# Written engine orders for the first 17 and last 16 slots of a matmul with decayed cumulative sum

## The chip, the cores and the metric

One core of one Trainium2 chip. The metric is device time in microseconds (us), the median of several executions. PE is the matrix engine (PEld its weight loads), DVE the vector engine, ACT the scalar engine, POOL GpSimd, SP the engine that issues the stores.

## The reference

```python
# x: (16, 2048, 1024), w: (1024, 1024), decay: (1024,), all float32
xw = x @ w
out[:, 0, :] = xw[:, 0, :]
for t in range(1, 2048):
    out[:, t, :] = decay * out[:, t - 1, :] + xw[:, t, :]
```

## The kernel before

The 16 x 2048 rows of x are 64 chunks of 512 rows. A chunk is loaded by GpSimd (cast to bf16), turned by DVE (32x32 transposes) and copied by ACT into the layout that PE reads (tile `xt`). Two chunks form a group; a *slot* is one block n of 128 output columns of a group, 2 x 8 matmuls of 512 columns into one PSUM tile of 1024. There are three such PSUM tiles, so PE can be at most two slots ahead of whoever empties the oldest. Each slot's recurrence runs over time inside the tile. A *direct* slot is one DVE scan over all 1024 steps. A *paired* slot combines two neighbouring steps so that DVE scans only 512, at the price of work on ACT and GpSimd:

```python
        def pair(self):          # "P"
            ...
            pin(nc.scalar.copy(out=self.xs, in_=self.ps))
            g = self.decayed(self.ps[:, 0:T:2])          # ACT: times decay; PSUM is free after it
            ... # first element of so: memset, or the state of the chunk before
            pin(nc.gpsimd.tensor_tensor(
                out=self.xs[:, 1:T:2], in0=g, in1=self.xs[:, 1:T:2], op=ALU.add))
        def scan(self):          # "S": DVE, 512 steps from xs, or 1024 steps straight from PSUM
            ...
        def complete(self):      # "C": ACT decays the odd steps, GpSimd adds the even ones; keep the state
            ...
        def back(self):          # "B": DVE turns the result; after the last of four blocks, store()
            ...
```

Every fourth slot is direct (from PSUM), the others are paired; only in the last eight slots, of one chunk each, is every second direct, and the last but one too. One rule orders the engines, slot after slot, start and end like the middle:

```python
    steps = {2: (3, 3, 4), 3: (4, 5, 5), 4: (7, 8, 10)}    # turn and copies of chunks 2, 3, 4
    def behind(new):
        if new is not None: new.pair()
        before = waiting[-1] if waiting else None
        if before is not None and before.paired: before.scan()
        if new is not None and not new.paired: new.scan()
        if before is not None: before.complete()
        ...                       # then back() of the slot before, or of the one before that
    slots = [(g, n) for g in groups[:-1] for n in range(K)]
    slots += [(groups[-1], n) for n in range(R)]            # R = 4, K = 8
    slots += [([c], n) for c in groups[-1] for n in range(R, K)]
```

All engines run strictly in the order written: `pin` keeps the program's order.

Of the kernel before, what the change touches and what calls it, by code (L numbers as in the profile page):

```python
# [25 lines left out]
def kernel(  # L26
# [7 lines left out]

# [102 lines left out]
    class Tile:  # L137
# [3 lines left out]
        def __init__(self, g, n, ps, ot):  # L141
            self.b, self.t0 = chunks[g[0]]
            self.T = TL * len(g)
            self.n, self.ps, self.ot = n, ps, ot
            self.final = g == [nch - 1]
            if len(g) == 2:
                self.paired = n % R != R - 1
            else:
                self.paired = n % 2 == 0 and not (self.final and n == K - 2)
# [65 lines left out]
        def back(self):  # L215
            T, n = self.T, self.n
            pin(nc.vector.transpose(  # L217
                out=self.ot[:, :, n % R * P:(n % R + 1) * P],
                in_=self.so[:, 2:T + 2].rearrange("p (i t) -> p i t", t=P)))
            if self.final:  # L220
                if n % 2:
                    self.store(n - 1, n + 1)
            elif n % R == R - 1:
                self.store(n + 1 - R, n + 1)

        def store(self, n0, n1):
            c0 = n0 % R * P
            size = (n1 - n0) * P
            for q in (0, 2, 1, 3):
# [9 lines left out]
    stage = {(0, 0): room[0][:, 0:size],  # L239
             (0, 1): room[0][:, size:size * 3 // 2].bitcast(BF16),  # L240
             (1, 0): room[1][:, 0:size // 2].bitcast(BF16),
             (1, 1): room[1][:, size // 2:size].bitcast(BF16)}

    def load_w(queue, h, e):
        for q in range(NQ):
            pin(queue.dma_start(  # L246
                out=stage[h, e][quad(q)].rearrange("p (m d) -> p m d", m=M),
                in_=_ap(w, [[2 * D, P], [2 * P * D, M], [1, CH]],
                        (q * CQ + e) * D + h * CH)))

    def settle(h, e, m, copy):
        src = stage[h, e][:, m * CH:(m + 1) * CH]
# [12 lines left out]
    load_w(nc.sync, 0, 0)  # L265
# [4 lines left out]
    for j0, j1 in halves:  # L270
        for q in range(NQ):
            load(0, q, j0, j1)
    load_w(nc.gpsimd, 0, 1)
    for j0, j1 in halves:
        for q in range(NQ):
            load(1, q, j0, j1)
    load_w(nc.gpsimd, 1, 0)
    load_w(nc.gpsimd, 1, 1)
    for q in range(NQ):
        load(2, q)  # L280

    def enter(c, j0, j1):
        turn(c, j0, j1)
        part(c, nc.vector.tensor_copy, 0, 2, j0, j1)
        part(c, nc.scalar.copy, 2, M, j0, j1)

    for e in range(2):
        for m in range(M):
            settle(0, e, m, nc.vector.tensor_copy if m < M // 2 else nc.scalar.copy)
        if e == 0:  # L290
            for j0, j1 in halves:
                enter(0, j0, j1)
    cols = const.tile([128, 2, P], FP32, name="cols")
    pin(nc.vector.transpose(out=cols, in_=rows))
    pin(nc.vector.tensor_copy(
        out=dec.rearrange("p (h r) -> p h r", h=2), in_=cols[:, :, 0:R]))
    pin(nc.vector.tensor_tensor(out=dec2[:, 0:K], in0=dec, in1=dec, op=ALU.mult))
    for j0, j1 in halves:
        enter(1, j0, j1)
    for m in range(M):  # L300
        settle(1, 0, m, nc.vector.tensor_copy)


    agenda = {}
    loads = []

    def at(step, f, *args):
        agenda.setdefault(step, []).append(lambda: f(*args))
# [6 lines left out]
    for m in range(M):  # L315
        at(0, settle, 1, 1, m, nc.vector.tensor_copy)
    steps = {2: (3, 3, 4), 3: (4, 5, 5), 4: (7, 8, 10)}
    for gi, g in enumerate(groups):
        for l, c in enumerate(g):
            if c > 1:  # L320
                ahead = (-7, -6, -4) if l else (-11, -10, -8)
                when = steps.get(c, [gi * K + s for s in ahead])
                at(when[0], turn_and_load, c)
                at(when[1], part, c, nc.scalar.copy, 0, 2)
                at(when[2], part, c, nc.scalar.copy, 2, M)

    waiting = []

    def behind(new):

        if new is not None:
            new.pair()
        before = waiting[-1] if waiting else None
        if before is not None and before.paired:
            before.scan()
        if new is not None and not new.paired:
            new.scan()
        if before is not None:
            before.complete()
        waiting.append(new)  # L340
        if len(waiting) == 4:
            waiting.pop(0)
        for tl, lag in ((waiting[0] if len(waiting) == 3 else None, True),
                        (before, False)):
            if tl is not None and tl.paired == lag:
                tl.back()

    loads.extend((c, q) for c in (3, 4) for q in range(NQ))
    slots = [(g, n) for g in groups[:-1] for n in range(K)]
    slots += [(groups[-1], n) for n in range(R)]  # L350
    slots += [([c], n) for c in groups[-1] for n in range(R, K)]
    for step, (g, n) in enumerate(slots):
        T = TL * len(g)
        if n % R == 0:
            ot = ot_tile(NJ * len(g))
        if step == 0:
# [9 lines left out]
            for j0, j1 in halves:  # L366
                for i in range(2):
# [20 lines left out]
        for f in agenda.pop(step, []):  # L388
            f()
# [34 lines left out]
```

## Time and profile before

| | before |
|---|---|
| time, median (range) | 928.25 us (928.22 to 928.48) |
| span of the profiled run | 926.5 us |
| PE busy | 893.3 us (96%) |
| first real matmul, last matmul's end | 12.81, 912.47 |
| waits of PE between 20 and 77 us | 11.6 us |
| DVE's last transpose ends | 918.62 |

The lines behind this table are in the prediction. How to read them: a timeline line is start, length, engine, source line, operation, output<-inputs, shapes, count; in brackets stands how long the engine stood idle before and what ended it. A line of the stretches is the window, its length, then busy time (and count) of PE, PEld, DVE, ACT, POOL, then PE's granted clock (1 is full), DMA share (1 is all 16 engines busy) and GB/s.

### The profile page before, as it was taken

To read this page: it belongs to the slowest core of one execution; us is meant where nothing else is said; L and a number is where in the kernel's file an instruction comes from. 1 tells how busy PE (TensorE), PEld (TensorE's weight loads), DVE (VectorE), ACT (ScalarE), POOL (GpSimd) and SP (SyncE) were. 2 spreads that over 40 slices of the span, in tenths; PEclk is the share of its full clock that TensorE was granted. 3 is DMA by queue.
4 is the path that set the end of the run, shared out by engine and by line. 5 is a ranking of instruction groups with operands and counts; after the bars stand their busy time and mean duration, and the time that the engine had idled before them with its cause. 6 is when DMAs were issued, how large, how long until landed. Compare 5 with 4: busy or idle time off the path is not lost. (4 is left out here: it accounts for less than half of the span.)

```text
span 926.5 us, 11865 instructions
## 1 busy us (share of the span) xinstructions
PE 893.3 (96%) x4080; PEld 408.1 (44%) x4162; DVE 827.9 (89%) x608; ACT 686.2 (74%) x937; POOL 666.6 (72%) x760
## 2 busy tenths in 40 slices
PE   8789999999999999999999999999999999999993
PEld 4334444444444444444444444444444444444441
DVE  4779999999999999999999999999999999999876
ACT  3478787787787787787777777777778778778751
POOL 7678877777776777777777777777777787785561
PEclk9999999999999999999999999999999999999997
DMA  9999999999999999999999999999999999999667
GB/s 184 146 190 229 215 226 247 252 248 242 262 230 222 236 226 222 236 228 222 234 231 220 233 231 223 237 225 229 229 229 225 232 234 222 230 228 193 144 168 181
DMA packets 406124, 204.74 MB, mean 221 GB/s; under 512 B 12848, under 2 KB 405552, under 8 KB 406064
## 3 DMA queue, kind: packets, MB, share of 16 engines
q1 hardware_dynamic: 269040, 135.29, 59.2%
q0 software_dynamic: 137024, 68.70, 55.4%
q8 instruction: 32, 0.52, 0.2%
q14 instruction: 28, 0.23, 0.1%
HBM read 138.42 MB, written 134.22 MB: 294 GB/s over the span
## 5 line engine op out<-in xcount | busy, mean ns | idle before, releaser
L127 PE MATMUL ps<-xt,wsb 128*128 128x512 bf16 (+1 forms) x4018 | 879.1, 378 | 18.0 <-DVE so L196 5.3
L127 PEld LDWEIGHTS <-wsb 128*128 128x128 bf16 x4128 | 404.2, 98 | 496.8 <-issue 18.6
L176 POOL TENSOR_TENSOR xs<-h,xs 128x512 f32<-128x512 f32 x192 | 247.4, 1288 | 206.0 <-ACT h L160 95.4
L170 ACT COPY xs<-ps 128x1024 f32<-128x1024 f32 x192 | 193.0, 1005 | 163.7 <-PE ps L127 155.5
L217 DVE STREAM_TRANSPOSE ot<-so 128x1024 f32<-128x1024 f32 (+1 forms) x260 | 302.4, 1201 | 2.5 <-POOL so L210 1.7
L210 POOL TENSOR_TENSOR so<-h,xs 128x512 f32<-128x512 f32 x192 | 246.5, 1284 | 34.8 <-ACT h L160 22.4
L124 ACT COPY xt<-xw 128x2048 bf16<-128x2048 bf16 (+1 forms) x128 | 240.0, 1876 | 15.1 <-DVE xw L116 15.1
L160 ACT ACTIVATE h<-so,dec 128x512 f32<-128x512 f32 x192 | 147.8, 770 | 39.3 <-DVE so L182 35.7
L106 POOL DMA_DIRECT2D xb<-in_x_dram x264 | 174.4, 661 | 2.3 <-POOLq L408 0.9
L182 DVE TENSOR_TENSOR_SCAN so<-dec,keep,xs 128x512 f32<-128x512 f32 (+1 forms) x96 | 121.3, 1264 | 34.4 <-POOL xs L176 34.2
L182 DVE TENSOR_TENSOR_SCAN so<-dec,xs 128x512 f32<-128x512 f32 x96 | 117.3, 1223 | 38.0 <-POOL xs L176 34.7
L116 DVE STREAM_TRANSPOSE xw<-xb 128x2048 f32<-128x2048 f32 (+1 forms) x66 | 146.6, 2221 | 4.3 <-DMA xb<-in_x_dram 4.3
L160 ACT ACTIVATE h<-ps,dec 128x512 f32<-128x512 f32 x192 | 132.5, 690 | 0.0
L196 DVE TENSOR_TENSOR_SCAN so<-dec,keep,ps 128x1024 f32<-128x1024 f32 (+1 forms) x34 | 75.7, 2228 | 0.0
L196 DVE TENSOR_TENSOR_SCAN so<-dec,ps 128x1024 f32<-128x1024 f32 x31 | 70.1, 2261 | 0.0
L213 ACT COPY keep<-so 128x1 f32<-128x1 f32 x132 | 24.8, 188 | 0.0
L175 ACT COPY so<-keep 128x1 f32<-128x1 f32 x96 | 18.4, 191 | 0.0
L262 PE MATMUL spare<-idle 128*128 128x512 bf16 x34 | 10.3, 479 | 1.2 <-DVE idle L259 1.2
L173 POOL MEMSET so<- 128x1 f32 x96 | 11.3, 117 | 0.0
L246 POOL DMA_DIRECT2D ot<-in_w_dram x12 | 6.7, 560 | 4.2 <-DMA xb<-in_x_dram 2.7
L253 DVE COPY wsb<-ot 128x512 bf16<-128x512 bf16 x10 | 5.4, 595 | 2.8 <-DMA ot<-in_w_dram 2.8
L253 ACT ACT_TABLE_LOAD x1 | 1.3, 1283 | 8.8 <-DMA ot<-in_w_dram 8.8
(18 smaller groups left out, 23.6 us busy)
## 6 DMA issues: line engine op xcount, KB each, us to landing
out_dram<-ot SPq DMA_DIRECT2D x252, 512.0 KB, 10.3
xb<-in_x_dram POOLq DMA_DIRECT2D x248, 256.0 KB, 7.5
xb<-in_x_dram POOLq DMA_DIRECT2D x16, 128.0 KB, 6.1
ot<-in_w_dram POOLq DMA_DIRECT2D x12, 128.0 KB, 5.0
ot<-in_w_dram SPq DMA_DIRECT2D x4, 256.0 KB, 5.2
out_dram<-ot SPq DMA_DIRECT2D x4, 256.0 KB
out_dram<-ot SPq DMA_DIRECT2D x8, 128.0 KB, 3.0
rows<-in_decay_dram SPq DMA_DIRECT2D x4, 1.0 KB
```

The source lines that it names most:

```text
L106: pin(nc.gpsimd.dma_start(out=xb_of[c][quad(q), j0:j1], in_=_ap(x, [[D, P], [P * D, j1 - j0], [1, CQ]], (b * S + t0 + j0 * P) * D + q * CQ)))
L116: pin(nc.vector.transpose(out=dst.rearrange("p (m j i) -> p j m i", m=M, i=P)[:, j0:j1], in_=src.rearrange("p (j m c) -> p j m c", m=M, c=P)))
L124: pin(copy(out=xt_of[c][:, m0:m1, :, j0 * P:j1 * P], in_=src))
L127: pin(nc.tensor.matmul(out=ps[:, t0:t1], lhsT=wsb[:, k, n].rearrange("p q i -> p (q i)"), rhs=xt[:, k // 2, k % 2, t0:t1], start=(k == 0 a ...
L160: pin(nc.scalar.activation(out=h, in_=src, func=mybir.ActivationFunctionType.Copy, scale=dec[:, self.n:self.n + 1]))
L170: pin(nc.scalar.copy(out=self.xs, in_=self.ps))
L176: pin(nc.gpsimd.tensor_tensor(out=self.xs[:, 1:T:2], in0=g, in1=self.xs[:, 1:T:2], op=ALU.add))
L182: pin(nc.vector.tensor_tensor_scan(out=so[:, 3:T + 2:2], data0=dec2[:, n:n + 1].to_broadcast([128, T // 2]), data1=self.xs[:, 1:T:2], init ...
L196: pin(nc.vector.tensor_tensor_scan(out=so[:, t:t + size], data0=dec[:, n:n + 1].to_broadcast([128, size]), data1=ps, initial=before, op0=A ...
L210: pin(nc.gpsimd.tensor_tensor(out=so[:, 2:T + 2:2], in0=h, in1=self.xs[:, 0:T:2], op=ALU.add))
L213: pin(nc.scalar.copy(out=self.keep, in_=so[:, T + 1:T + 2]))
L217: pin(nc.vector.transpose(out=self.ot[:, :, n % R * P:(n % R + 1) * P], in_=self.so[:, 2:T + 2].rearrange("p (i t) -> p i t", t=P)))
```

## The change

The intent is to win the waits at the start and shorten the tail, both of which the one rule for the middle does not suit. The core of the diff:

```diff
-    load_w(nc.sync, 0, 0)                       # first weight block: 1 MB of f32 on SP
+    load_w(nc.sync, 0, 0, 0, M // 2)            # half of it on SP; the other half, cast, on GpSimd ("U0")
-                for i in range(2):              # chunk 1 in half chunks for two heads (blocks 0, 1)
+                for i in range(3):              # ... for three
-            if len(g) == 2:
-                self.paired = n % R != R - 1
-            else:
-                self.paired = n % 2 == 0 and not (self.final and n == K - 2)
+            self.paired = n % R != R - 1
-    slots += [(groups[-1], n) for n in range(R)]
-    slots += [([c], n) for c in groups[-1] for n in range(R, K)]
+    slots += [([c], n) for c in groups[-1] for n in range(K)]
+    flips = (0, 1, -2, -15, -8)                 # slots that change between paired and direct
+    agenda = {
+        -99: "M0 M1 U0 U1 M2 M3 U2 U3 L L L W0 w1 E0 F0 G0 w3 W2 E1 F1 G1 W4 w5 W6 w7 E2 F2 D G2 E3 F3 G3 W8 W9 W10 W11",
+        0: "w12 L L w13 P0 S0",
+        1: "w14 L P1 L",
+        2: "S1 W15 P2 B0 S2",
+        3: "T2 L S3 C0 C1 C2",
+        4: "L P4 X2 L Y2 L B2 T3 B1 L",
         ... (slots 5 to 15)
+        16: "L P16 B14 B15 Y6 L L",
+        -16: "P-16 B-17 S-16 C-16 C-17",
+        -15: "P-15",
+        -14: "S-15 B-18 B-16 P-14",
         ... (slots -13 to -3)
+        -2: "P-2 S-2 C-4 C-3 B-4",
+        -1: "B-3 P-1 S-1 B-2 C-5 B-1 C-1 C-2",
+    }
```

P, S, C, B are the four parts of a slot; L loads a quarter chunk; T turns a chunk on DVE, X and Y are its copies on ACT; W copies a weight piece on DVE, w on ACT; M, E, F, G load, turn and copy half chunks; D prepares the decays. Slot -1 is the last one. P of a direct slot is nothing. All other slots keep the old rule.

More of the change, by code (lines that the diff above doesn't have):

```diff
@@ L137, with __init__ @@
     class Tile:
-        def __init__(self, g, n, ps, ot):
+        def __init__(self, g, n, ps, ot, there):
             self.b, self.t0 = chunks[g[0]]
             self.T = TL * len(g)
-            self.n, self.ps, self.ot = n, ps, ot
+            self.n, self.ps, self.ot, self.there = n, ps, ot, there
             self.final = g == [nch - 1]
-            if len(g) == 2:
-                self.paired = n % R != R - 1
-            else:
-                self.paired = n % 2 == 0 and not (self.final and n == K - 2)
+            self.paired = n % R != R - 1
+            if len(tiles) in flips or len(tiles) - len(slots) in flips:
+                self.paired = not self.paired
             self.so = ring(sb, "so", 4, [128, 2 * TL + 2])
@@ L219, in back @@
                 in_=self.so[:, 2:T + 2].rearrange("p (i t) -> p i t", t=P)))
-            if self.final:
-                if n % 2:
-                    self.store(n - 1, n + 1)
-            elif n % R == R - 1:
-                self.store(n + 1 - R, n + 1)
+            self.there.add(n)
+            size = 2 if self.final and n >= R else R
+            n0 = n // size * size
+            if self.there.issuperset(range(n0, n0 + size)):
+                self.store(n0, n0 + size)
         def store(self, n0, n1):
@@ L238, with load_w @@
     size = M * CH
-    stage = {(0, 0): room[0][:, 0:size],
-             (0, 1): room[0][:, size:size * 3 // 2].bitcast(BF16),
-             (1, 0): room[1][:, 0:size // 2].bitcast(BF16),
-             (1, 1): room[1][:, size // 2:size].bitcast(BF16)}
-    def load_w(queue, h, e):
+    stage = {(0, 0, 0): room[0][:, 0:size // 2],
+             (0, 0, M // 2): room[0][:, size // 2:size * 3 // 4].bitcast(BF16),
+             (0, 1, 0): room[0][:, size:size * 3 // 2].bitcast(BF16),
+             (1, 0, 0): room[1][:, 0:size // 2].bitcast(BF16),
+             (1, 1, 0): room[1][:, size // 2:size].bitcast(BF16)}
+    def load_w(queue, h, e, m0=0, m1=M):
         for q in range(NQ):
             pin(queue.dma_start(
-                out=stage[h, e][quad(q)].rearrange("p (m d) -> p m d", m=M),
-                in_=_ap(w, [[2 * D, P], [2 * P * D, M], [1, CH]],
-                        (q * CQ + e) * D + h * CH)))
+                out=stage[h, e, m0][quad(q)].rearrange("p (m d) -> p m d", m=m1 - m0),
+                in_=_ap(w, [[2 * D, P], [2 * P * D, m1 - m0], [1, CH]],
+                        (q * CQ + m0 * 2 * P + e) * D + h * CH)))
     def settle(h, e, m, copy):
-        src = stage[h, e][:, m * CH:(m + 1) * CH]
+        m0 = M // 2 if (h, e) == (0, 0) and m >= M // 2 else 0
+        src = stage[h, e, m0][:, (m - m0) * CH:(m - m0 + 1) * CH]
         pin(copy(out=wcols[:, 2 * m + e, h],
@@ L269, with load_half, load_part, settle_one @@
             in_=_ap(decay, [[P, R], [CH, 2], [1, P]], q * CR)))
-    for j0, j1 in halves:
+    cols = const.tile([128, 2, P], FP32, name="cols")
+    def load_half(i):
         for q in range(NQ):
-            load(0, q, j0, j1)
-    load_w(nc.gpsimd, 0, 1)
-    for j0, j1 in halves:
-        for q in range(NQ):
-            load(1, q, j0, j1)
-    load_w(nc.gpsimd, 1, 0)
-    load_w(nc.gpsimd, 1, 1)
-    for q in range(NQ):
-        load(2, q)
-    def enter(c, j0, j1):
-        turn(c, j0, j1)
-        part(c, nc.vector.tensor_copy, 0, 2, j0, j1)
-        part(c, nc.scalar.copy, 2, M, j0, j1)
-    for e in range(2):
-        for m in range(M):
-            settle(0, e, m, nc.vector.tensor_copy if m < M // 2 else nc.scalar.copy)
-        if e == 0:
-            for j0, j1 in halves:
-                enter(0, j0, j1)
-    cols = const.tile([128, 2, P], FP32, name="cols")
-    pin(nc.vector.transpose(out=cols, in_=rows))
-    pin(nc.vector.tensor_copy(
-        out=dec.rearrange("p (h r) -> p h r", h=2), in_=cols[:, :, 0:R]))
-    pin(nc.vector.tensor_tensor(out=dec2[:, 0:K], in0=dec, in1=dec, op=ALU.mult))
-    for j0, j1 in halves:
-        enter(1, j0, j1)
-    for m in range(M):
-        settle(1, 0, m, nc.vector.tensor_copy)
-    agenda = {}
-    loads = []
-    def at(step, f, *args):
-        agenda.setdefault(step, []).append(lambda: f(*args))
+            load(i // 2, q, *halves[i % 2])
+    def load_part(i):
+        load_w(nc.gpsimd, *((0, 0, M // 2, M), (0, 1), (1, 0), (1, 1))[i])
+    def settle_one(i, copy):
+        settle(i // 8, i // 4 % 2, i % 4, copy)
+    def decays(i):
+        pin(nc.vector.transpose(out=cols, in_=rows))
+        pin(nc.vector.tensor_copy(
+            out=dec.rearrange("p (h r) -> p h r", h=2), in_=cols[:, :, 0:R]))
+        pin(nc.vector.tensor_tensor(out=dec2[:, 0:K], in0=dec, in1=dec, op=ALU.mult))
+    slots = [(g, n) for g in groups[:-1] for n in range(K)]
+    slots += [([c], n) for c in groups[-1] for n in range(K)]
+    tiles = []
     def turn_and_load(c):
@@ L313, in turn_and_load @@
             loads.extend((c + 3, q) for q in range(NQ))
-    for m in range(M):
-        at(0, settle, 1, 1, m, nc.vector.tensor_copy)
-    steps = {2: (3, 3, 4), 3: (4, 5, 5), 4: (7, 8, 10)}
-    for gi, g in enumerate(groups):
-        for l, c in enumerate(g):
-            if c > 1:
-                ahead = (-7, -6, -4) if l else (-11, -10, -8)
-                when = steps.get(c, [gi * K + s for s in ahead])
-                at(when[0], turn_and_load, c)
-                at(when[1], part, c, nc.scalar.copy, 0, 2)
-                at(when[2], part, c, nc.scalar.copy, 2, M)
@@ L327 @@
-    waiting = []
-    def behind(new):
-        if new is not None:
-            new.pair()
-        before = waiting[-1] if waiting else None
-        if before is not None and before.paired:
-            before.scan()
-        if new is not None and not new.paired:
-            new.scan()
-        if before is not None:
-            before.complete()
-        waiting.append(new)
-        if len(waiting) == 4:
-            waiting.pop(0)
-        for tl, lag in ((waiting[0] if len(waiting) == 3 else None, True),
-                        (before, False)):
-            if tl is not None and tl.paired == lag:
-                tl.back()
@@ L348 @@
-    loads.extend((c, q) for c in (3, 4) for q in range(NQ))
-    slots = [(g, n) for g in groups[:-1] for n in range(K)]
-    slots += [(groups[-1], n) for n in range(R)]
-    slots += [([c], n) for c in groups[-1] for n in range(R, K)]
+    loads = [(c, q) for c in (2, 3, 4) for q in range(NQ)]
+    deeds = {
+        "P": lambda s: tiles[s % len(slots)].pair(),
+        "S": lambda s: tiles[s % len(slots)].scan(),
+        "C": lambda s: tiles[s % len(slots)].complete(),
+        "B": lambda s: tiles[s % len(slots)].back(),
+        "T": turn_and_load,
+        "X": lambda c: part(c, nc.scalar.copy, 0, 2),
+        "Y": lambda c: part(c, nc.scalar.copy, 2, M),
+        "x": lambda c: part(c, nc.vector.tensor_copy, 0, 2),
+        "y": lambda c: part(c, nc.vector.tensor_copy, 2, M),
+        "W": lambda i: settle_one(i, nc.vector.tensor_copy),
+        "w": lambda i: settle_one(i, nc.scalar.copy),
+        "M": load_half,
+        "U": load_part,
+        "E": lambda i: turn(i // 2, *halves[i % 2]),
+        "F": lambda i: part(i // 2, nc.vector.tensor_copy, 0, 2, *halves[i % 2]),
+        "G": lambda i: part(i // 2, nc.scalar.copy, 2, M, *halves[i % 2]),
+        "f": lambda i: part(i // 2, nc.vector.tensor_copy, 2, M, *halves[i % 2]),
+        "D": decays,
+        "L": lambda i: load(*loads.pop(0)) if loads else None,
+    }
@@ new lines @@
+    agenda = {
[5 more added lines that the diff above has]
+        4: "L P4 X2 L Y2 L B2 T3 B1 L",
+        5: "P5 C3 X3 L S4",
+        6: "B3 L Y3 S5 L P6 C5 C4 T4",
+        7: "S7 S6 X4 L C7 C6 B5 B4 B7",
+        8: "",
+        9: "P8 B6 S8 P9 L L T5 C8",
+        10: "P10 L L S9 L C9 L B8",
+        11: "X5 S10 L C10 S11 B9",
+        12: "P12 L B11 B10 C11 Y4",
+        13: "P13 S12 T6 Y5 C12 L",
+        14: "S13 P14 C13 L B12 L L",
+        15: "S15 X6 S14 C14 B13",
+        16: "L P16 B14 B15 Y6 L L",
+        -16: "P-16 B-17 S-16 C-16 C-17",
+        -15: "P-15",
+        -14: "S-15 B-18 B-16 P-14",
+        -13: "P-13 S-14 S-13 B-15",
+        -12: "P-12",
+        -11: "B-13 C-15 P-11 S-12 C-13 S-11 C-14 C-12",
+        -10: "P-10 B-14 C-11",
+        -9: "P-9 S-9 B-12",
+        -8: "S-10 P-8 S-8 B-11",
+        -7: "C-10 C-8 C-9 P-7 B-9",
+        -6: "P-6 B-10 S-7 C-7 B-8",
+        -5: "P-5 S-6 S-5",
+        -4: "C-6 B-7 B-5 P-4 B-6",
+        -3: "P-3 S-4 S-3",
+        -2: "P-2 S-2 C-4 C-3 B-4",
+        -1: "B-3 P-1 S-1 B-2 C-5 B-1 C-1 C-2",
+    }
@@ new lines, with usual @@
+    flips = (0, 1, -2, -15, -8)
+    later = {10: ["Y4"]}
+    for c in range(5, nch):
+        first = c // 2 * K
+        ahead = (7, 6, 4) if c % 2 else (11, 10, 8)
+        for letter, a in zip("TXY", ahead):
+            later.setdefault(first - a, []).append(f"{letter}{c}")
+    def usual(s):
+        paired = [t.paired for t in tiles]
+        do = [f"P{s}"] if paired[s] else []
+        if paired[s - 1]:
+            do.append(f"S{s - 1}")
+        if not paired[s]:
+            do.append(f"S{s}")
+        do.append(f"C{s - 1}")
+        if paired[s - 2]:
+            do.append(f"B{s - 2}")
+        if not paired[s - 1]:
+            do.append(f"B{s - 1}")
+        return do + later.get(s, []) + ["L"] * (2 if len(loads) > NQ else 1)
@@ L352, with perform @@
+    def perform(do):
+        for deed in do:
+            deeds[deed[0]](int(deed[1:] or 0))
+    perform(agenda[-99].split())
     for step, (g, n) in enumerate(slots):
@@ L354 @@
         if n % R == 0:
-            ot = ot_tile(NJ * len(g))
+            ot, there = ot_tile(NJ * len(g)), set()
         if step == 0:
@@ L375 @@
                 ps = (spare, second)
-            if n >= 2:
+            if n >= 3:
                 for k in range(K):
@@ L386 @@
                     matmul(ps[:, l * TL:(l + 1) * TL], n, k, xt_of[c])
-        behind(Tile(g, n, ps, ot))
-        for f in agenda.pop(step, []):
-            f()
-        for _ in range(2 if len(loads) > NQ else 1):
-            if loads:
-                load(*loads.pop(0))
-    behind(None)
-    behind(None)
-    assert not agenda and not loads
+        tiles.append(Tile(g, n, ps, ot, there))
+        left = step - len(slots)
+        do = agenda.get(step, agenda.get(left) if left >= -2 * K else None)
+        perform(usual(step) if do is None else do.split())
+    assert not loads
 _INS = ['x', 'w', 'decay']
```

## The prediction

> **What bounds the kernel now**
>
> I read the shares first, then the stretches, then the matrix engine's own order of time, its waits, and last the tail.
>
> ```profile
> PE 893.3 (96%) x4080; PEld 408.1 (44%) x4162; DVE 827.9 (89%) x608; ACT 686.2 (74%) x937; POOL 666.6 (72%) x760
> ```
>
> PE is busy for 893.3 of 926.5 us, so about 33 us can be won at the very most. Where they lie is shown by the table of stretches (stretch, length, busy PE, PEld, DVE, ACT, POOL, then granted clock, DMA share, GB/s):
>
> ```profile
> 30.00:40.00 10.00, 6.00 (x28) 2.52 (x26) 7.48 (x8) 3.92 (x8) 7.35 (x10) 1.00 1.12 142
> 40.00:50.00 10.00, 8.06 (x29) 3.32 (x30) 9.20 (x7) 6.44 (x7) 3.86 (x7) 0.83 0.86 131
> ...
> 300.00:400.00 100.00, 99.53 (x456) 45.38 (x464) 92.57 (x66) 77.54 (x107) 75.13 (x86) 1.00 1.19 227
> ```
>
> In the middle PE is busy 99.5%; between 30 and 50 us it is idle for almost 6 of 20 us and its clock sinks to 0.83 in the second half. PE's timeline from the start up to there (start, length, last the idle time before it and its releaser):
>
> ```profile
> 23.57 8.81 PE L127 MATMUL ps<-xt,wsb 128*128 128x256 bf16 x47 [0.81 <-DVE xt L124]
> 34.13 3.61 PE L127 MATMUL ps<-xt,wsb 128*128 128x512 bf16 x16 [1.75 <-ACT h L160]
> 40.25 1.12 PE L127 MATMUL ps<-xt,wsb 128*128 128x512 bf16 x4 [2.51 <-DVE so L196]
> 41.60 3.95 PE L127 MATMUL ps<-xt,wsb 128*128 128x512 bf16 x11 [0.22 <-issue]
> 47.01 3.83 PE L127 MATMUL ps<-xt,wsb 128*128 128x512 bf16 x17 [1.46 <-ACT h L160]
> 52.93 6.92 PE L127 MATMUL ps<-xt,wsb 128*128 128x512 bf16 x30 [2.08 <-ACT xt L124]
> 61.03 13.97 PE L127 MATMUL ps<-xt,wsb 128*128 128x512 bf16 x63 [1.19 <-DVE so L196]
> 76.61 33.61 PE L127 MATMUL ps<-xt,wsb 128*128 128x512 bf16 x152 [1.60 <-DVE so L196]
> ```
>
> Slots 5, 6, 7, 8, 10 and 14 (a slot is one output column block of 16 matmuls) each start with a wait, always for a PSUM tile that ACT or DVE has not emptied, or for an xt tile that ACT has not copied. After 76.61 there is none. The whole work is 64 chunks x 64 = 4096 matmuls of 512 columns; 14 slots (224) are over at 76.61 and the last ends at 912.47, so 3872 took 835.86 us, 215.9 ns each. The first 224 need 48.4 us at that pace but took 76.61 - 12.81 (the first real matmul) = 63.8. So 15.4 us are lost between 12.8 and 76.6, of which the six waits after 32 us are 10.6, the wait at 23.57 is 0.8, and the slow clock some 1.8 (slot 6 took 5.3 us against 3.45).
>
> Behind the last matmul come 926.5 - 912.47 = 14.0 us of tail:
>
> ```profile
> 912.63 2.42 DVE L196 TENSOR_TENSOR_SCAN so<-dec,keep,ps 128x512 f32<-128x512 f32 x2
> 914.97 1.28 DVE L217 STREAM_TRANSPOSE ot<-so 128x512 f32<-128x512 f32 x2
> 916.18 1.24 DVE L196 TENSOR_TENSOR_SCAN so<-dec,keep,spare 128x512 f32<-128x512 f32 x1
> 917.34 1.28 DVE L217 STREAM_TRANSPOSE ot<-so 128x512 f32<-128x512 f32 x2
> ```
> ```profile
> 900.00:905.00 5.00, 4.95 (x24) 2.28 (x24) 5.00 (x4) 1.52 (x4) 1.99 (x2) 1.00 0.36 103
> ...
> 913.00:915.00 2.00, 0.00 (x0) 0.00 (x0) 2.00 (x3) 0.33 (x1) 0.73 (x1) 0.96 1.02 264
> ...
> 924.00:925.00 1.00, 0.00 (x0) 0.00 (x0) 0.00 (x0) 0.00 (x0) 0.00 (x0) 0.50 1.00 212
> ```
>
> DVE is 6.15 us behind PE when it ends (918.62). After that the DMA engines still work at share 1.00 up to 925: the last pair of chunks (4.2 MB) is written from 905 on, after five almost empty microseconds. So the tail is a store backlog on top of a DVE backlog.
>
> **What the Trainium skill says**
>
> "TensorE: Matmul & The Clock Gate", section "Back-to-back issue gap", gives N/2.4 + 2.5 ns for a warm matmul, 215.8 for 512 columns; the trace's 215.9 agrees, so the middle holds nothing to win. The same page, "What's actually happening", says that PE falls to half clock after an idle window of about 3.4 us. Here the clock fell with two waits of 1.75 and 2.51 us some 6 us apart, each shorter than that, so short waits in a row are not safe by this trace. "GPSIMD Engine Reference", section "1. Specifications", has GpSimd share its SBUF interfaces with VectorE in 2-port modes; the weight copies on DVE agree: 4 took 1.21 us at 24.14, but 3 took 3.49 us at 26.88 beside GpSimd's adds. "Perfetto Trace Analysis", "Optimization Strategy", speaks of kernels with several regimes; start, middle and tail are three here, and the change works on the first and last.
>
> **The change part by part**
>
> Costs are start-to-start times from the timeline: paired slot: ACT 0.90 + 0.60 (copy, decayed evens) to free PSUM, GpSimd 1.25, DVE scan 1.20, ACT 0.67, GpSimd 1.25, DVE transpose 1.16. Direct slot: DVE scan 2.24, transpose 1.16. Turning a chunk: DVE 2.23; its two ACT copies 1.85 each. A load: GpSimd 0.65.
>
> Start of loading. Half of the first weight block (0.52 MB of f32 rows) leaves the SP queue and becomes four more GpSimd loads: 4 x 0.65 = 2.6 us of issue. In before, GpSimd stood 2.7 us at its ninth load, until a first x piece had landed (8.7 us); with half the weight traffic ahead of it (0.52 MB at about 200 GB/s = 2.6 us) that wait should go. The two cancel. The first real matmul cannot come before the warm-up matmuls end at 11.5; then k = 4 and 6 wait for the late weights (issue 6 to 8.6, landing 5 us later, copy 0.6: about 13.9). Half 1 then starts at 15.6, as in before (15.55). Gain here 0, at best 1.5.
>
> Three heads in half chunks. Head 2 is taken with heads 0 and 1: eight more half matmuls (0.87 us) fill PE while the second half of chunk 1 lands. Waits of 0.22 and 0.81 go; three heads are finished at 26.1 instead of some 27.1.
>
> Slots 0 to 16. Slots 0 and 1 become direct: 2 x (2.24 - 1.20) = 2.1 us more DVE, but 4 x 1.25 us of GpSimd and 2 x 2.17 of ACT fall away, and so do two chains of five engines at the moment when the ring of three PSUM tiles is full. Three weight copies go from DVE to ACT (they cost DVE over 1.1 each beside GpSimd). Chunk turns come sooner: chunk 2 is turned behind the scan of slot 2, not at 41.26. Walking the written orders through: DVE has the weights at 25.3, scans slot 0 to 27.55 and slot 1 to 29.8; PE runs slot 3's second part at 27.6 (idle 1.5) and slot 4 at 29.9 (idle 0.5) to 33.3. Slot 2 is read by ACT at 28.7 to 30.2, so slot 5 follows at once, to 36.8. DVE: slot 2's scan ends 32.8, turn of chunk 2 35.0, slot 3's two scans 37.4: slot 6 starts 37.5 (idle 0.7), slot 7 at 40.9, slot 8 at 44.4 (chunk 3's copies end on ACT 43.9 and 45.7, in time for its later matmuls). Slots 9 to 13 find their tiles free at 47.2, 51.2, 54.6, 56.1 and 60.4, each before PE is there (47.9, 51.3, 54.8, 58.2, 61.7). Slot 14 waits for slot 11's direct scan: 66.2 against 65.1, idle 1.2. Slot 14 starts at 66.3, against 76.6: gain 10.3 us. The idle left is 3.9 us in four pieces, the longest 1.5, so the clock should hold. DVE's scan of slot 15 then ends 4.5 us behind PE's slot; in before this lag was 6.3, so the middle keeps the gain.
>
> Last 16 slots. Columns 0 to 3 of the last pair go chunk by chunk: four slots of 1024 become eight of 512. A pair scan costs DVE 2 x 0.63 for 1.20, a direct one 2 x 1.20 for 2.24, transposes 2 x 0.62 for 1.16: under 1 us in all, beside PE. DVE's sum is 7 direct x 1.85 + 9 paired x 1.3 = 24.7 us against 16 x 1.72 = 27.6 of PE: it keeps up. Counted from PE's end: scans of the last but three end at -2.0, of -3 at -0.7, direct -2 at 0.5, transposes 1.7, direct -1 at 3.0, two transposes 4.4. So DVE ends 4.4 after PE instead of 6.15: 1.8. More counts that chunk 62's first half, 1 MB, is stored some 15 us before PE's end, not 6 to 7, its second at about -8, chunk 63's first half at -2.7 (0.5 MB per pair after it). At 225 GB/s 1 MB takes 4.7 us, so only the last 0.5 MB (2.3 us) lies behind the last transpose, with issue, landing and end some 5.2 us in place of 7.9. Tail 14.0 - 9.6 = 4.4.
>
> Sum: 10.3 + 4.4 = 14.7, held back to 14: 928.25 - 14 = 914.
>
> **The rivals**
>
> The start's bound turns to DVE or ACT order. Strict written orders make every late item hold all behind it; a chunk landing late (7.5 us median, up to 13.5 in the first 30 us) stops the turn and every scan behind it. For it: DVE is 92 to 100% busy from 60 us on. Against: the loads for chunks 2 and 3 are issued earlier than they are turned. It would give back 3 to 6 us: 918 to 920.
>
> The new GpSimd loads delay the first pass by 2 to 3 us and PE, idle between the warm-up and the late weights, loses its clock: about 918. Against: the smaller SP transfer in front.
>
> The store queue stays the tail's bound: if 256-byte rows write slower than 225 GB/s, the tail gains only 2: 916.5.
>
> All waits vanish: the start then gives up to 15.4, the tail 6: about 907.
>
> **Range and chances**
>
> Start 6 to 13, tail 2 to 5.5: 910 to 919 in 8 of 10. 2% needs 18.6 us, more than my sum and nearly all idle time: chance 0.08. Slower needs a new stall in each of the 31 groups, whose order is unchanged: 0.01.
>
> **What would show each step right or wrong**
>
> PE's waits between 27 and 70 us should sum to some 4 us, none over 2, clock 1.00 in 40 to 50; slot 14 should begin near 66. The first turn of chunk 2 should be near 33. PE's end should be near 902, DVE's last transpose 4 to 5 us later, and the DMA share should be high well before PE's end. I am wrong if PE still waits for xt or PSUM more than 6 us in all, if the first pass begins after 17, or if the stores still run at share 1.00 for more than 4 us behind DVE's end.

## The result and the profile after

| | before | after |
|---|---|---|
| time, median (range) | 928.25 us (928.22 to 928.48) | 915.0 us (914.06 to 915.91) |
| span of the profiled run | 926.5 | 912.5 |
| slot 14 starts | 76.61 | 65.71 |
| PE's last matmul ends | 912.47 | 901.58 |
| DVE's last transpose ends | 918.62 | 905.55 |

The ratio of times is 0.9857 (95% interval 0.984 to 0.9874). A ratio here is the mean time of one kernel's runs over that of the other's of the same rounds, so it is not quite the ratio of the medians. The change is 1.4% faster, which is within 2%.

The page of the kernel after, its engine shares:

```profile
PE 891.3 (98%) x4088; PEld 408.5 (45%) x4170; DVE 826.0 (91%) x613; ACT 685.8 (75%) x950; POOL 664.4 (73%) x764
```

Its stretches, at the start and in the middle:

```profile
30.00:40.00 10.00, 9.14 (x43) 4.08 (x42) 9.22 (x7) 7.51 (x11) 7.03 (x9) 1.00 1.31 168
40.00:50.00 10.00, 9.95 (x48) 4.49 (x47) 10.00 (x8) 9.23 (x12) 7.05 (x9) 1.00 1.05 141
...
300.00:400.00 100.00, 99.53 (x456) 45.30 (x463) 92.57 (x66) 78.50 (x108) 73.75 (x84) 1.00 1.20 234
```

Busy PE went from 6.00 to 9.14 and from 8.06 to 9.95 in the first two, the clock from 0.83 to 1.00 in the second; the middle is as it was. Its PE timeline from the second chunk on:

```profile
20.64 5.70 PE L126 MATMUL ps<-xt,wsb 128*128 128x256 bf16 x48 [0.39 <-DVE xt L123]
27.59 1.89 PE L126 MATMUL ps<-xt,wsb 128*128 128x512 bf16 x7 [1.25 <-DVE so L194]
29.77 7.07 PE L126 MATMUL ps<-xt,wsb 128*128 128x512 bf16 x32 [0.29 <-DVE so L194]
37.69 27.79 PE L126 MATMUL ps<-xt,wsb 128*128 128x512 bf16 x125 [0.86 <-DVE so L194]
65.71 44.62 PE L126 MATMUL ps<-xt,wsb 128*128 128x512 bf16 x202 [0.23 <-DVE so L194]
```

Four waits are left after 26 us, before slots 3, 4, 6 and 14, 2.63 us in all; each is for a direct scan of DVE (L194). The tail, first DVE's last instructions, then the stretches:

```profile
900.75 1.25 DVE L194 TENSOR_TENSOR_SCAN so<-dec,keep,ps 128x512 f32<-128x512 f32 x1
901.92 1.28 DVE L215 STREAM_TRANSPOSE ot<-so 128x512 f32<-128x512 f32 x2
903.12 1.24 DVE L194 TENSOR_TENSOR_SCAN so<-dec,keep,spare 128x512 f32<-128x512 f32 x1
904.28 1.27 DVE L215 STREAM_TRANSPOSE ot<-so 128x512 f32<-128x512 f32 x2
```
```profile
880.00:885.00 5.00, 4.95 (x23) 2.25 (x23) 5.00 (x6) 3.47 (x12) 2.21 (x3) 1.00 0.30 69
885.00:890.00 5.00, 5.00 (x25) 2.27 (x24) 4.77 (x8) 3.11 (x12) 3.61 (x5) 1.00 0.86 207
...
895.00:900.00 5.00, 5.00 (x25) 2.28 (x24) 4.20 (x6) 3.04 (x8) 2.68 (x4) 1.00 1.02 264
...
909.00:911.00 2.00, 0.00 (x0) 0.00 (x0) 0.00 (x0) 0.00 (x0) 0.00 (x0) 0.50 0.91 196
```

DVE ends 3.97 us behind PE (before: 6.15). From 885 to 911 the stores run almost without a gap, but from 880 to 885 the DMA engines had been nearly idle (69 GB/s). From DVE's end to the end of the span it is 6.95 us (before: 7.9). The tail behind the last matmul is thus 3.97 + 6.95 = 10.9 us, in place of 14.0.

### The profile page after: what moved, and what is told of

Read it like the earlier page. It is cut to its first block, busy times and chain, and to the rows that moved or that the text cites. A ratio compares the mean times of both kernels' runs of the same rounds, so it can differ in the third digit from the quotient of the medians. Undisturbed runs are those within 1.5% of the kernel's fastest.

```text
span 912.5 us, 11926 instructions
## 1 busy us (share of the span) xinstructions
PE 891.3 (98%) x4088; PEld 408.5 (45%) x4170; DVE 826.0 (91%) x613; ACT 685.8 (75%) x950; POOL 664.4 (73%) x764
## 4 chain that ended last, share of the span: by engine, by line
PE 90%; DMA 3%; POOL 2%; issue 2%; DVE 2%; ACT 1%; SPq 0%; DVEq 0%; POOLq 0%
PE ps L126 90%; DMA xb<-in_x_dram 2%; POOL xb L105 1%; DMA ot<-in_w_dram 1%; DVE so L194 1%; DVE xw L115 1%; POOL ot L245 1%; PE spare L126 0%; DMA out_dram<-ot 0%; DVE so L180 0%; POOL so L208 0%; ACT xt L123 0%; DVE ot L215 0%; POOL xs L174 0%; ACT xs L168 0%
## 5 line engine op out<-in xcount | busy, mean ns | idle before, releaser
L174 POOL TENSOR_TENSOR xs<-h,xs 128x512 f32<-128x512 f32 (+1 forms) x193 | 245.3, 1271 | 195.5 <-ACT h L158 88.3
L168 ACT COPY xs<-ps 128x1024 f32<-128x1024 f32 (+1 forms) x193 | 191.6, 993 | 158.8 <-PE ps L126 149.3
L208 POOL TENSOR_TENSOR so<-h,xs 128x512 f32<-128x512 f32 (+1 forms) x193 | 244.3, 1266 | 34.5 <-ACT h L158 18.1
L158 ACT ACTIVATE h<-so,dec 128x512 f32<-128x512 f32 (+1 forms) x193 | 147.1, 763 | 36.0 <-DVE so L180 32.1
L180 DVE TENSOR_TENSOR_SCAN so<-dec,xs 128x512 f32<-128x512 f32 x94 | 114.8, 1222 | 31.3 <-POOL xs L174 28.2
L158 ACT ACTIVATE h<-ps,dec 128x512 f32<-128x512 f32 (+1 forms) x193 | 131.8, 683 | 0.0
L194 DVE TENSOR_TENSOR_SCAN so<-dec,ps 128x1024 f32<-128x1024 f32 x33 | 74.5, 2261 | 0.0
L194 DVE TENSOR_TENSOR_SCAN so<-dec,keep,ps 128x1024 f32<-128x1024 f32 (+1 forms) x33 | 73.4, 2225 | 0.0
L126 PE MATMUL spare<-xt,wsb 128*128 128x512 bf16 (+1 forms) x43 | 11.2, 359 | 0.1
L253 ACT COPY wsb<-ot 128x512 bf16<-128x512 bf16 x6 | 3.4, 615 | 5.7 <-DMA ot<-in_w_dram 5.7
```

The lines of the kernel that those rows point to most:

```text
L126: pin(nc.tensor.matmul(out=ps[:, t0:t1], lhsT=wsb[:, k, n].rearrange("p q i -> p (q i)"), rhs=xt[:, k // 2, k % 2, t0:t1], start=(k == 0 a ...
L158: pin(nc.scalar.activation(out=h, in_=src, func=mybir.ActivationFunctionType.Copy, scale=dec[:, self.n:self.n + 1]))
L174: pin(nc.gpsimd.tensor_tensor(out=self.xs[:, 1:T:2], in0=g, in1=self.xs[:, 1:T:2], op=ALU.add))
L180: pin(nc.vector.tensor_tensor_scan(out=so[:, 3:T + 2:2], data0=dec2[:, n:n + 1].to_broadcast([128, T // 2]), data1=self.xs[:, 1:T:2], init ...
L194: pin(nc.vector.tensor_tensor_scan(out=so[:, t:t + size], data0=dec[:, n:n + 1].to_broadcast([128, size]), data1=ps, initial=before, op0=A ...
L208: pin(nc.gpsimd.tensor_tensor(out=so[:, 2:T + 2:2], in0=h, in1=self.xs[:, 0:T:2], op=ALU.add))
```

## The experiments

The first four, the next four and the last four runs each shared a chip and the runs of the kernel before (medians 928.45, 928.27 and 928.49 us). All but one give a correct result. This table reads each kernel's own profiled run: the start of slot 14 says what the start was worth, the last three columns make up the tail.

| run | median us | ratio to before | slot 14 starts | PE ends | DVE end behind PE | end behind DVE |
|---|---|---|---|---|---|---|
| before | 928.25 | 1 | 76.61 | 912.47 | 6.15 | 7.9 |
| after | 915.0 | 0.9857 | 65.71 | 901.58 | 3.97 | 6.95 |
| start_only | 917.93 | 0.9888 | 66.11 | 901.97 | 6.15 | 7.7 |
| tail_only | 925.36 | 0.9969 | 77.60 | 913.47 | 4.06 | 7.0 |
| regroup_usual | 917.72 | 0.9881 | 68.62 | 904.49 | 5.80 | 6.7 |
| less_stored | 914.08 | 0.9845 | 66.46 | 902.32 | 3.98 | 5.4 |
| paired_first | 920.88 | 0.9919 | 72.68 | 908.54 | 3.98 | 6.9 |
| usual_start | 921.06 | 0.9921 | 72.30 | 908.16 | 3.98 | 6.9 |
| two_heads | 915.1 | 0.986 | 66.39 | 902.25 | 3.98 | 6.8 |
| whole_w | 914.55 | 0.9852 | 65.37 | 901.23 | 4.07 | 6.7 |
| paired_w15 | 919.72 | 0.9902 | 71.61 | 908.52 | 3.99 | 6.9 |
| early_back | 914.77 | 0.9851 | 67.49 | 903.36 | 3.98 | 5.5 |
| better_start | 917.19 | 0.9886 | 66.4 | 904.57 | 3.98 | 6.9 |
| combined | 923.55 | 0.9947 | 66.0 | 904.02 | 4.27 | 13.6 |

The 66.4 and 66.0 are worked out: no wait stands before slot 14 there, so it is the start of slot 10 plus four slots of 3.45 us. A caution on all of them: the first part of chunk 1 came to PE at 20.6 to 22.6 us in these profiles although the loading is the same in most, so slot 14 moves by up to about 2 us from run to run, and differences of one us between kernels are not to be read from the medians.

### start_only: the start of after, the tail of before

```diff
-            self.paired = n % R != R - 1
+            self.paired = n % R != R - 1 if len(g) == 2 else n % 2 == 0 and not (self.final and n == K - 2)
-    slots += [([c], n) for c in groups[-1] for n in range(K)]
+    slots += [(groups[-1], n) for n in range(R)]
+    slots += [([c], n) for c in groups[-1] for n in range(R, K)]
-        (agenda lines -16 to -1)
-    flips = (0, 1, -2, -15, -8)
+    flips = (0, 1)
```

> Loading, three heads, direct first slots and written orders of slots 0 to 16 as in the changed kernel; the last 16 slots as in the kernel before. Theory (start and tail gains are separate and add): the start is worth 10.9 us (slot 14 at 65.7 instead of 76.6), so 917.4 us, with the matrix engine's end near 901.6 and a tail of 14.0. Rival (the start only moves work into the tail): above 920.

Measured 917.93 us: 10.5 below before's 928.45. PE's end at 901.97 and a tail of 13.8 are what the theory expected.

### tail_only: the start of before, the tail of after

The edit takes back the loading, the third head, the written orders of slots 0 to 16 and the flips of slots 0 and 1, and keeps the rest.

```diff
-    flips = (0, 1, -2, -15, -8)
-    later = {10: ["Y4"]}
+    flips = (-2, -15, -8)
+    later = {0: ["W12", "W13", "W14", "W15"], 3: ["T2", "X2"], 4: ["Y2", "T3"], 5: ["X3", "Y3"],
+             7: ["T4"], 8: ["X4"], 10: ["Y4"]}
```

> The start as in the kernel before, the last 16 slots as in the changed kernel. Theory: only the tail shrinks, from 14.0 to 10.9 us behind the last matmul, so 925.1. Rival (gains depend on each other): within 1 us of 928.25 or below 923.

Measured 925.36 us, 3.1 below before. The two parts give 10.5 + 3.1 = 13.6 us; the whole change gives 13.25. They are separate and add.

### regroup_usual: chunk by chunk at the end, but in the usual order

```diff
-        (agenda lines -16 to -1)
-    flips = (0, 1, -2, -15, -8)
+    flips = (0, 1)
```

> As the changed kernel, but the last 16 slots, still chunk by chunk, take the usual order and no flips. Theory (the tail is bound by the stores, which the chunk-by-chunk slots bring forward): most of the tail's gain stays, 915 to 916. Rival (the written order, which lets the vector engine end sooner behind the last matmul, is the gain): as without any tail change, 917.4 or more.

Measured 917.72 us, as start_only (917.93). In its trace the tail is 12.5 us, 1.3 shorter than start_only's 13.8 and 1.6 longer than after's 10.9, and slot 14 came 2.5 us later than start_only's. By the total time nothing is left of this step; by the trace of one run each it is worth 1.3 us, and the written order with its flips 1.6, all of it because DVE ends 3.97 instead of 5.80 us behind PE. The theory that the grouping carries most of the tail's gain is not borne out: the rival holds by the times. But the run does not price the grouping alone. The rule for single chunks went with it, so that two of the last eight slots are direct here and five in start_only, and slot -2 is paired. What the grouping is worth with the same direct slots was not tried.

### less_stored: 1 MB of the last groups is not stored (wrong)

```diff
-            if self.there.issuperset(range(n0, n0 + size)):
+            if self.there.issuperset(range(n0, n0 + size)) and not (
+                    self.T == TL and not self.final and n < R):
```

> Wrong result on purpose: as the changed kernel, but the first half of the columns of the last chunk but one (1 MB of 134) is not stored. Theory (in the tail the DMA engines are the bound from some 17 us before the last matmul on): 1 MB at 225 GB/s is 4.7 us of backlog, and the tail shrinks from 10.9 to 8.5 to 9.5 us, where issue and landing of the last store bind: 912.5 to 913.6. Rival (the vector engine's last transposes bind): 915.0, unchanged.

Measured 914.08 us, 0.9 below after; the ranges (913.08 to 914.75 and 914.06 to 915.91) overlap. In the trace DVE ends 3.98 us behind PE, as in after, and the end comes 5.4 us behind DVE instead of 6.95 (6.7 to 7.0 in the eight traces that have after's last slots). So the 1 MB taken out is worth 1.5 us of after's tail; DVE's order, and the 5.4 us that the last stores need once DVE is done, are the rest. The tail of 9.4 us is within the expected range, the time is half a us above it.

### paired_first: slots 0 and 1 paired

```diff
-        0: "w12 L L w13 P0 S0",
-        1: "w14 L P1 L",
-        2: "S1 W15 P2 B0 S2",
-        3: "T2 L S3 C0 C1 C2",
+        0: "P0 S0 w12 L L w13",
+        1: "P1 w14 L L",
+        2: "S1 W15 P2 C0 C1 S2 B0",
+        3: "T2 L S3 C2",
-    flips = (0, 1, -2, -15, -8)
+    flips = (-2, -15, -8)
```

> As the changed kernel, but slots 0 and 1 paired as in the kernel before, with ACT reading them ahead of its three weight copies and their completion ahead of the first transpose. Theory (two more chains over five engines keep DVE from slot 3's scans, so that slot 6 waits): slot 3 and 4 start sooner (near 25.7 and 27.5), but slot 6 waits 3 to 5 us and starts near 39, the clock dips, 917 to 919. Rival (the orders alone are the gain, and ACT empties the first tiles sooner): 915 or less.

Measured 920.88 us, 5.9 above after: worse than either theory. The PE timeline of this run, and two groups of lines of its timeline of all engines:

```profile
30.49 3.18 PE L126 MATMUL ps<-xt,wsb 128*128 128x512 bf16 x14 [1.94 <-ACT h L158]
37.07 5.75 PE L126 MATMUL ps<-xt,wsb 128*128 128x512 bf16 x18 [3.40 <-DVE wsb L253]
44.02 27.79 PE L126 MATMUL ps<-xt,wsb 128*128 128x512 bf16 x128 [1.20 <-DVE so L194]
```
```profile
32.98 4.03 DVE L253 COPY wsb<-ot 128x512 bf16<-128x512 bf16 x1
...
33.10 1.30 POOL L174 TENSOR_TENSOR xs<-h,xs 128x512 f32<-128x512 f32 x1
...
34.35 2.51 POOL L208 TENSOR_TENSOR so<-h,xs 128x512 f32<-128x512 f32 x2
```

One weight copy on DVE lasts 4.03 us, from just before to just after three GpSimd adds that follow each other without a gap; in after the same copy, W15, takes 0.26 us with GpSimd still idle. PE waits 3.40 us for it, and the clock falls (0.87 between 30 and 40 us).

### paired_w15: the same, with that copy on ACT

```diff
-        1: "P1 w14 L L",
-        2: "S1 W15 P2 C0 C1 S2 B0",
+        1: "P1 w14 w15 L L",
+        2: "S1 P2 C0 C1 S2 B0",
```

> As paired_first, but the fourth of the late weight copies is done by ACT too. There it took the vector engine 4.03 us while GpSimd ran three adds behind one another, and the matrix engine waited 3.4 us for it. Theory A (that copy, held up by GpSimd's adds, is most of what paired first slots cost): the 3.4 us wait and the clock dip go, 916 to 918. Theory B (the longer chain over five engines delays slot 3's scans anyway): the wait moves to slot 6, 920 to 921.

Measured 919.72 us, 1.2 below paired_first and 4.7 above after. The PE timeline:

```profile
32.01 8.75 PE L126 MATMUL ps<-xt,wsb 128*128 128x512 bf16 x32 [2.04 <-ACT h L158]
43.18 27.79 PE L126 MATMUL ps<-xt,wsb 128*128 128x512 bf16 x125 [2.42 <-DVE so L194]
```

The 3.4 us wait for the copy is gone, but slot 6 now waits 2.42 us for slot 3's scans, and the 32 matmuls of slots 4 and 5 take 8.75 us against 7.07 in after, so the clock was down again (0.83 from 30 to 40 us). The time lies between the two theories, nearer to B: ahead of slot 3's scans DVE stood idle for 2.53, 2.69 and 1.37 us, each time for a GpSimd add of a paired slot, where after has one such wait of 0.67 us. This trace shows the slowest of the four runs (921.16 us): chunk 1 came 2.0 us later than in after, and the clock had been down once before (0.66 from 15 to 20 us). Part of the 2.04 us at slot 4 is this order's own doing: ACT stood behind two weight copies that had not landed, with slot 1's tile full. A better order of paired slots was not sought, so the 4.7 us is the cost of this one.

### usual_start: direct first slots, but the usual order from slot 0 on

```diff
-        (agenda lines 0 to 16)
-    later = {10: ["Y4"]}
+    later = {0: ["W12", "W13", "W14", "W15"], 3: ["T2", "X2"], 4: ["Y2", "T3"], 5: ["X3", "Y3"],
+             7: ["T4"], 8: ["X4"], 10: ["Y4"]}
```

> As the changed kernel with slots 0 and 1 direct, three heads and the split weight load, but slots 0 to 16 in the usual order of the kernel before. Theory (written orders and direct slots both are needed): most waits of before return, 919 to 924. Rival (the direct slots are the gain and the orders only trim): within 2 us of 915.

Measured 921.06 us, 6.1 above after, as expected. Its PE timeline:

```profile
42.59 3.83 PE L126 MATMUL ps<-xt,wsb 128*128 128x512 bf16 x17 [0.98 <-ACT h L158]
48.51 6.92 PE L126 MATMUL ps<-xt,wsb 128*128 128x512 bf16 x31 [2.08 <-ACT xt L123]
56.62 13.97 PE L126 MATMUL ps<-xt,wsb 128*128 128x512 bf16 x64 [1.19 <-DVE so L194]
72.30 37.93 PE L126 MATMUL ps<-xt,wsb 128*128 128x512 bf16 x175 [1.71 <-DVE so L194]
```

The last three waits are those of before at slots 8, 10 and 14 (there 2.08, 1.19 and 1.60). The two of before that went are those at slots 5 and 6 (1.75 and 2.51), and with them the dip of the clock. That the dip comes from these waits is not shown: tail_only has them too (1.75 and 2.52) and then one of 3.15, at a clock of 1.00 from 20 to 60 us. Nor did the dip cost before time of its own: from slot 6's start to slot 7's it took 6.76 us in before (40.25 to 47.01) and 6.77 in tail_only (40.88 to 47.65), so the wait for ACT had room for it, and the 1.8 us that the prediction counts for the slow clock were no separate loss. So the direct slots remove the early waits and the written order the later ones. Each alone keeps a part of the start's gain: 928.27 - 921.06 less the tail's 3.1 is 4.1 of 10.5 for the direct slots; for the written order it is 4.3 with paired_first and 5.7 (928.49 - 919.72 - 3.1) with paired_w15.

### two_heads and whole_w: the small parts of the start taken back

```diff
-                for i in range(3):
+                for i in range(2):
-            if n >= 3:
+            if n >= 2:
```
```diff
-    load_w(nc.sync, 0, 0, 0, M // 2)
+    load_w(nc.sync, 0, 0)
-        -99: "M0 M1 U0 U1 M2 M3 ...
+        -99: "M0 M1 U1 M2 M3 ...
```

> As the changed kernel, but two heads in half chunks as in the kernel before. Theory (slot 3 waits for the vector engine's scan of slot 0 in any case, until 27.6 in the trace of the changed kernel): 914.5 to 915.5, no change. Rival (the 0.9 us that the third head fills are a gain): 915.9.

> As the changed kernel, but the first weight block loaded whole as f32 rows on the SP queue. Theory (the first pass starts later, but the second weight half and chunk 1 land as before, and these set slot 0's scan at 25.3): 914.5 to 916. Rival (2.2 us later landing of the first x pieces moves everything): 917.

Measured 915.1 and 914.55 us: neither can be told from after. With two heads PE waits twice for chunk 1 (0.81 and 0.80 us), but slot 3 then waits only 0.40 us for slot 0's scan instead of 1.25. The third head fills time in which PE would wait anyway.

### early_back: an earlier transpose, so that stores start sooner

```diff
-        -16: "P-16 B-17 S-16 C-16 C-17",
+        -16: "P-16 B-17 B-18 S-16 C-16 C-17",
-        -14: "S-15 B-18 B-16 P-14",
+        -14: "S-15 B-16 P-14",
```

The written order holds the last transpose of the second last pair of chunks back until slot -14, and 2 MB of stores with it, while the DMA engines idle (the 69 GB/s above).

> As the changed kernel, but the last transpose of the pair of chunks before the last one (slot -18) comes in slot -16 and not in slot -14, so that its 2 MB of stores can start 2 us sooner, while the DMA engines are idle. Theory (the stores are 1.5 us of the tail's 10.9, by the run that stored 1 MB less): the time from the vector engine's end to the end goes from 7.0 to 5.5, 913.5 to 914.3. Rival (the later scan of slot -16 delays the vector engine's end as much): 915.

Measured 914.77 us, which cannot be told from after's 915.0. In the trace the end comes 5.5 us behind DVE instead of 6.95, as the theory said, and DVE's lag is unchanged (3.98). But in this profiled run chunk 1 came late (PE waited 1.53 us for it, in after 0.39) and slot 14 started at 67.49. So the tail's 1.5 us are seen in one trace, clear of the 6.7 to 7.0 of the eight traces without this edit, and not in the times.

### better_start and combined: two attempts at more

```diff
-        -99: "... G3 W8 W9 W10 W11",
+        -99: "... G3 w8 w9 w10 w11",
-        2: "S1 W15 P2 B0 S2",
-        3: "T2 L S3 C0 C1 C2",
+        2: "S1 W15 P2",
+        3: "S3 B0 S2 T2 L C0 C1 C2",
-        11: "X5 S10 L C10 S11 B9",
+        11: "X5 S11 S10 L C10 B9",
```

> As the changed kernel, but four weight copies ahead of slot 0's scan go to ACT, slot 3's scans come ahead of the first transpose, and slot 11's direct scan ahead of slot 10's. Theory (slot 0's scan waits for those copies, and slots 3, 4, 6 and 14 for the vector engine, 2.6 us in all): slot 3 starts 1.1 us sooner, the waits at slots 6 and 14 go, and the matrix engine is 1 to 2 us sooner at slot 16: 913 to 914. Rival (vector engine and ACT are full from 30 to 70 us, so that each wait taken away comes back later): 915.

Measured 917.19 us (916.32 to 922.36), 2.2 above after. The waits at slots 6 and 14 did go, and slot 3 waited 0.63 us instead of 1.25. The PE timeline and a DVE line of its timeline of all engines show where it came back:

```profile
52.55 28.14 PE L126 MATMUL ps<-xt,wsb 128*128 128x512 bf16 x126 [0.88 <-DVE so L194]
81.49 14.05 PE L126 MATMUL ps<-xt,wsb 128*128 128x512 bf16 x63 [0.80 <-DVE so L194]
96.33 13.97 PE L126 MATMUL ps<-xt,wsb 128*128 128x512 bf16 x62 [0.80 <-DVE so L194]
```
```profile
48.01 2.31 DVE L115 STREAM_TRANSPOSE xw<-xb 128x2048 f32<-128x2048 f32 x1 [1.93 <-DMA xb<-in_x_dram]
```

DVE's turn of chunk 4 starts at 48.01 instead of 45.37, after an idle wait of 1.93 us for the chunk's data. With slot 2's scan later, its completion on GpSimd is later (36.22 instead of 33.85), and chunk 4's loads, which stand behind it in the order, are issued later too (the last three from 39.41 instead of 37.03). Some 0.7 us of this is a later start: slot 0's scan began at 25.93 instead of 25.26. The rival holds: the waits came back, at slot 10 and then at slots 18 and 22.

combined adds early_back and issues the last four stores by SP and ACT in turn:

```diff
-                pin(nc.sync.dma_start(
+                queue = nc.scalar if self.final and n0 == K - 2 and q % 2 else nc.sync
+                pin(queue.dma_start(
```

> early_back and better_start together, and the last four stores issued by SP and ACT in turn instead of SP alone. Theory (the three gains add; two issuers save one issue time of 0.5 to 0.9 us): 911 to 913. Rival (the DMA engines, not the issue, bind at the end, and the start's gains are given back): 914 to 915.

Measured 923.55 us, 8.6 above after. The waits of SP from 880 us on, and the lines of its issues around the gap:

```profile
SPq L229 <- DMA out_dram<-ot: 11.0, 1, 11.0
```
```profile
896.72 3.04 SPq L229 DMA_DIRECT2D out_dram<-ot  x3
908.31 0.93 ACTq L229 DMA_DIRECT2D out_dram<-ot  x2
910.83 3.26 SPq L229 DMA_DIRECT2D out_dram<-ot  x4
```

SP stood once for 11.0 us waiting for a store to land, and goes on at 910.83, 2.5 us after ACT issued its two. In the built program the stores of both issuers take turns at the same eight completion counters, and ACT's two had been given theirs ahead of earlier stores of SP, which then had to wait for ACT's, issued at the very end. That is read from the program's waits and fits the trace. The kernel has them: ahead of the stores of the last chunk's first half SP waits for the value that ACT's first store gives its counter. Whether two issuers with separate counters would help was not tried.

## Why the prediction was right

The time was 915.0 us against 914 predicted, and the parts of the sum were 10.5 (start_only; predicted 10.3) and 3.1 (tail_only; predicted 4.4). The sum of 14.7 was 1.45 too large; that 914 is only 1 us off owes 0.7 to holding back, for which the prediction gives no reason.

- **Loading is worth nothing.** Right: whole_w is 914.55. GpSimd's wait of 2.71 us at its ninth load shrank to 0.39, as said, and half 1 of the first pass started at 14.89, predicted 15.6.
- **Three heads.** The heads were finished at 26.3, as walked through (26.1), but the step "Waits of 0.22 and 0.81 go" is no gain by itself, as two_heads shows, because slot 0's scan on DVE ends later in any case.
- **Slots 0 to 16.** The hand-walked times held to within 0.6 us at every wait: slots 3, 4, 6 and 14 predicted at 27.6, 29.9, 37.5, 66.3, measured 27.59, 29.77, 37.69, 65.71. The four predicted waits of 1.5, 0.5, 0.7 and 1.2 were 1.25, 0.29, 0.86 and 0.23, and the clock held. What made this work is that the engines ran their lists in the written order (DVE in after, from 25.26 to 38.7 us: S0 S1 W15 B0 S2 T2 S3 B2): with start-to-start times from the trace of before, every engine's list can be summed on paper. That direct slots are what frees the early ring is shown by paired_first, paired_w15 and usual_start; that the two halves of the start both count was not sized in the prediction. DVE's scan of slot 15 ended 5.45 us behind PE's slot, predicted 4.5 (before 6.3); the middle kept the gain all the same.
- **DVE behind PE.** Predicted 4.4, measured 3.97: 2.2 of the tail's 3.1 us, predicted 1.8.
- **The stores, the mis-sized term.** "only the last 0.5 MB (2.3 us) lies behind the last transpose, with issue, landing and end some 5.2 us in place of 7.9" measured 6.95: a gain of 0.9 us, predicted 2.7. When DVE ended, 1.09 MB were still to be moved, not 0.5 (1.38 in before). The working followed the last two chunks and left out the pair before them: its last transpose moves to slot -14 in the written order, so 2 MB came late onto the DMA engines, which were idle just before. less_stored (5.4) and early_back (5.5) show that without this backlog the 5.2 is about right, though 0.8 MB were still left in both. And "More counts that chunk 62's first half, 1 MB, is stored some 15 us before PE's end" is not borne out: the stores' part of the gain is 0.9 and DVE's 2.2, and regroup_usual, without the order and the flips, gave nothing in time and 1.3 us of tail in the trace.
- **The checks set beforehand.** Waits near 4 us with none over 2 (2.63, longest 1.25), clock 1.00, slot 14 near 66, PE's end near 902 (901.58): all passed. The chunk 2 turn "near 33" was at 32.87. The one that failed is "the stores still run at share 1.00 for more than 4 us behind DVE's end": they ran at 0.91 to 0.94 for 5.4 us. So the third rival was partly right, with a backlog of 1.5 us; and the last stores, whose rows are 256 bytes, did run below 225, at 196 to 207 GB/s after 905 us, against 264 from 895 to 900.
- **Lines read too freely.** Loads of x landing in "7.5 us median, up to 13.5 in the first 30 us": 7.5 is the median of the whole run; in the first 30 us the trace has 7.1, and 8.4 at most. The "five almost empty microseconds" before 905 had a DMA share of 0.36. Neither carries a sum.

## What to carry to other kernels

Where PE is full in the middle, look at the ends, and read each wait there as a full ring of buffers: find the engine that empties it, and give that engine the shortest chain first. When engines run in order, a slot-by-slot order can be checked on paper with start-to-start times from the trace; but walk every engine, the DMA queue too, from before the stretch that changes. An order tuned for one wait at a time gives it back elsewhere when two engines are already full, so run each step.

## What the Trainium skill lacked or had wrong

- "TensorE: Matmul & The Clock Gate", "What's actually happening": half clock after an idle window of some 3.4 us. In before the clock fell (0.83 from 40 to 50 us) with no wait longer than 2.51. In usual_start waits of up to 2.08 left it at 1.00 all through, and in tail_only waits of 1.75, 2.52 and 3.15 left it at 1.00 from 20 to 60 us. So the longest wait alone does not tell. The same page's "A second HAM failure mode" does have short idles between groups of matmuls make the clock fall and rise; it gives no length for them.
- The same page, "Back-to-back issue gap": the 215.8 ns of its formula agree with the 215.9 measured here; its sustained figure of about 131 ns for 512 columns does not.
- No page read here has it: a DVE copy can last as long as several GpSimd instructions in a row; the pages have one instruction of one engine wait for one of the other. A copy of 0.26 us took 4.03 us here, the whole length of three GpSimd adds, although its record starts 0.12 us before theirs (paired_first).
- No page read here has it: stores of two issuers can wait for each other through shared completion counters; SP stood 11.0 us in combined.
